# Two transformer blocks on one core: the order of the four products of a k-tile

## The chip, the cores and the metric

The kernel runs on one core of one Trainium2 chip. The metric is the device time of one execution in microseconds (us). TensorE (PE) does the matrix products, VectorE (DVE) and ScalarE (ACT) the elementwise work, and SyncE (SP) issues nearly all DMAs.

## The reference

Two transformer blocks follow each other on 256 tokens of width 2048, in float32. Nearly all the work is in products of the tokens with weight matrices:

```python
h = rmsnorm(x, norm_w[layer])
proj = h @ w_in[layer]
...
gm = jax.nn.sigmoid(h @ w_merge[layer] + b_merge[layer]).reshape(b, s, N_BRANCHES, D_MODEL)
merged = gm[:, :, 0] * y_a + gm[:, :, 1] * y_b
x = x + merged @ w_out[layer]
...
proj = xn @ w_in[l]
h = h + merged @ w_o[l]
hn = rmsnorm_2(h, ffn_norm_g[l])
up = causal_dwconv(hn @ w_up[l], ffn_conv_w[l], ffn_conv_b[l])
val, gt = jnp.split(up, 2, axis=-1)
h = h + (jax.nn.silu(gt) * val) @ w_down[l]
```

The first block has a pooling branch and a sparse attention, the second a convolution, a chunked attention and a memory attention, and a feed-forward part of width 5632. These parts are small beside the weight products.

## The kernel before

**Strips.** Each weight matrix is cut into strips of 256 output columns, and `stream` (L309) goes through all strips in one written-out list. A strip has one k-tile for each 128 rows of its matrix (16 for a matrix of 2048 rows; 2 to 24 occur). Weights arrive by DMA in granules of up to eight k-tiles (`raw` tiles). A step is up to four k-tiles of a granule: `split` (L349) has ACT round the raw weights to a `hi` tile (format fp32r, L168) and DVE compute `lo` = raw - hi (L172), two steps ahead of their use, into four `hi` and four `lo` buffers. The activations are split in the same way: a page `R` holds for a k-tile 256 columns of hi, one for each token, and behind them 256 columns of lo.

**The products.** In the mode "ws" (the weights stand in the array, the activations move through it) a k-tile has two halves `f` of 128 output columns each, with its own half `ps[:, f]` of the accumulator tile, 512 float32 columns. For each half there are two products, made by the helper `mm` (L204, so all of them are on L206): hi weights with all 512 columns of the page, and lo weights with its first 256. In this document "a hi" is the first of these, "a lo" the second. All k-tiles of a strip add into the same `ps`; `sum2` (L416) later adds the two column ranges of it. Two `ps` tiles take turns from strip to strip.

**The order.** The order on PE is the order in which the Python code calls `mm`; nothing reorders it (`manual_schedule`). `stream` issues a step's products, then calls `round` (L275), which lets the waiting epilogues and the attention jobs issue one piece each. In every k-tile but the last the order is hi, lo for half 0 and hi, lo for half 1. In a strip's last k-tile it is lo, hi, lo, hi, so that there two lo follow each other, and two hi follow each other where the next strip begins. The modes "as" (the activations stand, all products have 256 or 304 columns) and "cmp" are in the other branches of the same loop.

Of the kernel before, what the change touches and what calls it, by code (L numbers as in the profile page):

```python
# [72 lines left out]
class Builder:  # L73
# [235 lines left out]
    def stream(self, strips):  # L309
        steps, grans = [], []  # L310

        def granules(ss):
            for s in ss:
                kt = 0
                for ap, n in s.grans:
                    yield s, ap, n, kt
                    kt += n

        def order():
            for s in strips:  # L320
                if isinstance(s, Strip):
                    yield from granules([s])
                else:
                    runs = [granules(x) for x in s[:2]]
                    for i in s[2]:
                        yield next(runs[i])
        for s, ap, n, kt in order():
            for k0 in range(0, n, s.per):
                m = min(s.per, n - k0)
                steps.append((s, len(grans), k0, m, kt + k0, k0 + m >= n))  # L330
            grans.append((ap, n, s.width))
        raw, hl, loaded, done = {}, {}, 0, 0

        def cut(tile, n, w):
            return tile[:, 0:n * w].rearrange("p (k c) -> p k c", k=n)

        def load(most):
            nonlocal loaded
            while loaded < min(len(grans), most) and loaded - done < self.RAW:
                ap, n, w = grans[loaded]  # L340
                r = raw[loaded] = cut(self.t("raw", [128, 2048], self.RAW), n, w)
                if loaded:
                    self.dma(r[:, 0:n, :], ap)
                else:
                    self.dma(r[:, 0:4, :], ap[:, 0:4, :])
                    self.dma(r[:, 4:8, :], ap[:, 4:8, :])
                loaded += 1

        def split(j):  # L349
            nonlocal done  # L350
            s, g, k0, m, _, end = steps[j]
            h = cut(self.t("hi", [128, 1024], self.HL, F32R), m, s.width)
            l = cut(self.t("lo", [128, 1024], self.HL, F32R), m, s.width)
            self.split(h, l, raw[g][:, k0:k0 + m, :])
            hl[j] = h, l
            if end:
                del raw[g]
                done = g + 1

        for j in range(self.RAW):  # L360
            self.start_loads(j)
            load(j + 1)
        self.start_loads(self.RAW)
        for j in range(self.AHEAD):
            self.round()
            split(j)
        ended = None
        for j, (s, g, k0, m, kt, _) in enumerate(steps):
            if j + self.AHEAD < len(steps):
                split(j + self.AHEAD)  # L370
                load(len(grans))
            if kt == 0:
                self.drain(lambda: self.shared["ps"])
                s.ps = self.shared["ps"].popleft()
                if s.pre:
                    self.job(s.pre())
            self.drain(lambda: all(s.act(kt + q) is not None for q in range(m)))
            h, l = hl.pop(j)
            ps = s.ps
            for q in range(m):  # L380
                k = kt + q
                first, last = k == 0, k == s.nkt - 1
                x = s.act(k)
                if s.mode == "ws":
                    for f in range(2):
                        c = slice(f * 128, f * 128 + 128)
                        if last:
                            self.mm(ps[:, f, 0:256], l[:, q, c], x[:, 0:256], False, False)
                        self.mm(ps[:, f, :], h[:, q, c], x, first, last)
                        if not last:  # L390
                            self.mm(ps[:, f, 0:256], l[:, q, c], x[:, 0:256], False, False)
                elif s.mode == "as":
                    for f in range(2):
                        c, o = f * 128, ps[:, f, 0:s.width]
                        self.mm(o, x[:, c:c + 128], h[:, q, :], first, False)
                        self.mm(o, x[:, c:c + 128], l[:, q, :], False, False)
                        self.mm(o, x[:, 256 + c:384 + c], h[:, q, :], False, last)
                else:

                    if last:  # L400
                        self.mm(ps[0:60, 0, 0:256], x[:, 0:60], l[:, q, :], False, False)
                    self.mm(ps[0:120, 0, 0:256], x, h[:, q, :], first, last)
                    if not last:
                        self.mm(ps[0:60, 0, 0:256], x[:, 0:60], l[:, q, :], False, False)
            if ended is not None:
                self.job(ended)
                ended = None
            self.round()
            if kt + m == s.nkt:
                ended = s.epi(ps)  # L410
                if s.end:
                    s.end()
        self.job(ended)
        self.drain(lambda: not (self.epis or self.run or self.bg or self.fill))
# [1427 lines left out]
```

## Time and profile before

| | |
|---|---|
| median of 3 runs | 2566.55 us (2565.39 to 2566.99) |
| the profiled execution | 2566.05 us |
| its span, first to last instruction | 2564.3 us |
| PE busy | 2546.6 us, 99% |
| weight loads (PEld) busy | 2240.8 us, 87% |
| DVE busy | 1892.6 us, 74% |
| ACT busy | 1386.3 us, 54% |
| DMA | 481.24 MB, mean 188 GB/s |
| mean granted TensorE clock | 0.996 |

The span is the profiled execution's own; the 1.75 us between it and the execution's time lie around it. A busy share says how long an engine had at least one instruction in flight. PE's products overlap, and their ends are modelled, so what a product takes of PE's time is read from the starts.

### The profile page before, as it was taken

How to read it: one execution, taken by the hardware profiler on the slowest of the kernel's cores; microseconds unless marked ns; L12 is line 12 of the kernel's file. 1: busy time of each engine (PE TensorE's matmuls, PEld its weight loads, DVE VectorE, ACT ScalarE, POOL GpSimd, SP SyncE). 2: the span in 40 equal slices, each digit the busy share in tenths (PEclk: the TensorE clock that was granted, in tenths of full speed). 3: DMA queues.
4: the chain of work that ended last, by engine and by line, in shares of the span. 5: the costliest groups of instructions: out<-in, count | busy, mean ns of one | idle time of the engine just before them, and what ended most of it. 6: DMA issues, size and time to landing. Idle time of an engine off the chain costs nothing.

```text
span 2564.3 us, 37620 instructions
## 1 busy us (share of the span) xinstructions
PE 2546.6 (99%) x15126; PEld 2240.8 (87%) x15126; DVE 1892.6 (74%) x2990; ACT 1386.3 (54%) x2008; POOL 0.2 (0%) x4
## 2 busy tenths in 40 slices
PE   9999999999999999999999999999999999999997
PEld 7989888888888888888888888888888888888886
DVE  6687677777856667788888787677788764688764
ACT  6556555555554455555555445655555554455553
POOL 0000000000000000000000000000000000000000
PEclk9999999999999999999999999999999999999999
DMA  6757444444555566554555554555555555555553
GB/s 252 257 196 258 166 164 148 149 149 152 179 207 185 188 222 199 189 187 173 192 187 175 188 187 173 192 202 204 181 199 183 195 182 196 181 191 187 187 191 115
DMA packets 75632, 481.24 MB, mean 188 GB/s; under 512 B 8640, under 2 KB 8896, under 8 KB 20544
## 3 DMA queue, kind: packets, MB, share of 16 engines
q1 hardware_dynamic: 75024, 478.38, 52.9%
q8 instruction: 118, 1.93, 0.3%
q14 instruction: 58, 0.48, 0.1%
q10 hardware_dynamic: 432, 0.45, 0.1%
HBM read 472.50 MB, written 6.29 MB: 187 GB/s over the span
## 4 chain that ended last, share of the span: by engine, by line
PE 99%; DVE 1%; DMA 0%; ACT 0%; issue 0%; SPq 0%; DVEq 0%
PE ps L206 95%; PE A L206 2%; PE O L206 1%; PE A L216 1%; DMA raw<-in_w_mem 0%; DVE F L172 0%; DVE nq L172 0%; DVE lo L172 0%; ACT hi L168 0%; DVE F L187 0%; SPq L251 0%; DVE F L182 0%; DVE small L172 0%; ACT nq L168 0%; DVEq L1837 0%
## 5 line engine op out<-in xcount | busy, mean ns | idle before, releaser
L206 PE MATMUL ps<-R,hi 128*128 128x512 f32 x6480 | 2276.6, 396 | 2.2 <-ACT hi L168 2.2
L206 PE MATMUL ps<-R,lo 128*128 128x256 f32 x6480 | 1786.1, 281 | 0.5 <-DVE lo L172 0.5
L206 PEld LDWEIGHTS ps<-R,hi 128*128 128x128 f32 x6480 | 1208.7, 188 | 270.6 <-issue 3.2
L172 DVE TENSOR_TENSOR lo<-raw,hi 128x1024 fp32r<-128x1024 f32 (+1 forms) x878 | 1069.3, 1219 | 383.2 <-ACT hi L168 379.6
L206 PEld LDWEIGHTS ps<-R,lo 128*128 128x128 f32 x6480 | 1216.8, 188 | 18.8 <-DVE lo L172 1.0
L168 ACT ACTIVATE hi<-raw 128x1024 fp32r<-128x1024 f32 (+1 forms) x878 | 920.7, 1052 | 501.4 <-PE ps L206 386.5
L172 DVE TENSOR_TENSOR F<-ps,F 128x512 f32<-128x512 f32 (+1 forms) x226 | 155.0, 686 | 172.9 <-ACT F L168 158.6
L168 ACT ACTIVATE F<-ps 128x512 f32<-128x512 f32 (+1 forms) x210 | 124.8, 594 | 276.6 <-PE ps L206 276.4
L172 DVE TENSOR_TENSOR F<-F,F 128x512 f32<-128x512 f32 (+3 forms) x300 | 185.5, 620 | 8.7 <-ACT F L168 3.3
L182 DVE SCALAR_TENSOR_TENSOR F<-F,params,F 128x256 f32<-128x256 f32 (+2 forms) x424 | 188.4, 479 | 3.3
L206 PE MATMUL ps<-hi,R 128*128 128x256 f32 (+2 forms) x832 | 152.9, 281 | 0.1
L168 ACT ACTIVATE F<-F 128x256 f32<-128x256 f32 (+2 forms) x140 | 75.0, 535 | 117.2 <-DVE F L182 97.5
L206 PEld LDWEIGHTS ps<-hi,R 128*128 128x128 f32 (+1 forms) x832 | 129.7, 188 | 0.6 <-ACT hi L168 0.5
L168 ACT ACTIVATE F<-F,params 128x256 f32<-128x256 f32 x214 | 106.8, 545 | 31.8 <-DVE F L172 30.6
L206 PE MATMUL ps<-lo,R 128*128 128x256 f32 (+2 forms) x448 | 122.6, 280 | 0.0
L168 ACT ACTIVATE R<-F 128x256 fp32r<-128x256 f32 (+3 forms) x145 | 69.4, 490 | 54.8 <-DVE F L172 50.4
L206 PEld LDWEIGHTS ps<-lo,R 128*128 128x128 f32 (+1 forms) x448 | 80.6, 180 | 0.4
L172 DVE TENSOR_TENSOR R<-F,R 128x256 fp32r<-128x256 f32 (+3 forms) x129 | 62.1, 493 | 0.0
L182 DVE SCALAR_TENSOR_TENSOR F<-F,F 128x256 f32<-128x256 f32 (+1 forms) x112 | 60.7, 542 | 0.0
L168 ACT ACTIVATE R<-A 128x512 fp32r<-128x512 f32 (+2 forms) x56 | 29.8, 532 | 56.3 <-PE A L216 56.3
L172 DVE TENSOR_TENSOR R<-A,R 128x512 fp32r<-128x512 f32 (+2 forms) x56 | 34.0, 607 | 22.6 <-ACT R L168 22.6
L168 ACT ACTIVATE F<-F,mx 128x128 f32<-128x128 f32 (+1 forms) x96 | 42.7, 446 | 11.3 <-DVE mx L187 10.4
(101 smaller groups left out, 591.2 us busy)
## 6 DMA issues: line engine op xcount, KB each, us to landing
raw<-in_w_in SPq DMA_DIRECT2D x166, 1024.0 KB, 4.9
raw<-in_w_up SPq DMA_DIRECT2D x88, 1024.0 KB, 4.8
raw<-in_w_merge SPq DMA_DIRECT2D x32, 1024.0 KB, 4.8
raw<-in_w_down_a SPq DMA_DIRECT2D x24, 1024.0 KB, 4.8
raw<-in_w_nsa_out SPq DMA_DIRECT2D x16, 1024.0 KB, 4.9
raw<-in_w_out SPq DMA_DIRECT2D x16, 1024.0 KB, 5.3
raw<-in_w_o SPq DMA_DIRECT2D x16, 1024.0 KB, 4.8
raw<-in_w_down_b SPq DMA_DIRECT2D x16, 1024.0 KB, 4.8
```

The lines of the kernel that those rows point to most:

```text
L168: return self.nc.scalar.activation(out, in_, f, **k)
L172: return self.nc.vector.tensor_tensor(out, a, b, op=op)
L182: return self.nc.vector.scalar_tensor_tensor(out, a, s, b, op0=op0, op1=op1)
L206: return self.nc.tensor.matmul(out, l, r, start=start, stop=stop, skip_group_check=True)
L216: return self.nc.tensor.transpose(out, in_, self.ident[0:n, 0:n])
```

## The change

In the mode "ws" a k-tile's four products are now issued as hi for half 0, hi for half 1, lo for half 0, lo for half 1. This holds for the last k-tile of a strip as well, which had the lo ahead of the hi. The flag that opens an accumulation stays on the first k-tile's two hi, the one that closes it moves from the last k-tile's hi to its lo.

```diff
@@ -382,13 +382,11 @@
                 first, last = k == 0, k == s.nkt - 1
                 x = s.act(k)
                 if s.mode == "ws":
-                    for f in range(2):
-                        c = slice(f * 128, f * 128 + 128)
-                        if last:
-                            self.mm(ps[:, f, 0:256], l[:, q, c], x[:, 0:256], False, False)
-                        self.mm(ps[:, f, :], h[:, q, c], x, first, last)
-                        if not last:
-                            self.mm(ps[:, f, 0:256], l[:, q, c], x[:, 0:256], False, False)
+
+                    for w, n in ((h, 512), (l, 256)):
+                        for f in range(2):
+                            self.mm(ps[:, f, 0:n], w[:, q, f * 128:f * 128 + 128], x[:, 0:n],
+                                    first and n == 512, last and n == 256)
                 elif s.mode == "as":
```

The order of the instructions on PE, before, at the first products of the program (k-tile 0 of the first strip; `R_68` is the page of activations, and what a row waits for stands behind it):

```order
L206 MATMUL ps_120<-R_68,hi_175 128x512 [waits DVE_49,Activation_49]
L206 MATMUL ps_120<-R_68,lo_176 128x256 [waits DVE_49]
L206 MATMUL ps_120<-R_68,hi_175 128x512
L206 MATMUL ps_120<-R_68,lo_176 128x256
L206 MATMUL ps_120<-R_68,hi_175 128x512
```

And the same place on PE after the change:

```order
L206 MATMUL ps_120<-R_68,hi_175 128x512 [waits DVE_49,Activation_49]
L206 MATMUL ps_120<-R_68,hi_175 128x512
L206 MATMUL ps_120<-R_68,lo_176 128x256 [waits DVE_49]
L206 MATMUL ps_120<-R_68,lo_176 128x256
L206 MATMUL ps_120<-R_68,hi_175 128x512 x2
```

The wait for DVE, which makes the lo tile, moved from the second product to the third.

On PE before, where a strip ends (its last two k-tiles, page `R_75`) and the next one begins (page `R_68`, the other `ps` tile):

```order
L206 MATMUL ps_121<-R_75,hi_320 128x512
L206 MATMUL ps_121<-R_75,lo_321 128x256
L206 MATMUL ps_121<-R_75,hi_320 128x512
L206 MATMUL ps_121<-R_75,lo_321 128x256 x2
L206 MATMUL ps_121<-R_75,hi_320 128x512
L206 MATMUL ps_121<-R_75,lo_321 128x256
L206 MATMUL ps_121<-R_75,hi_320 128x512
L206 MATMUL ps_120<-R_68,hi_344 128x512 [waits Activation_49]
L206 MATMUL ps_120<-R_68,lo_345 128x256 [waits DVE_49]
```

The same place on PE after the change:

```order
L206 MATMUL ps_121<-R_75,hi_320 128x512 x2
L206 MATMUL ps_121<-R_75,lo_321 128x256 x2
L206 MATMUL ps_121<-R_75,hi_320 128x512 x2
L206 MATMUL ps_121<-R_75,lo_321 128x256 x2
L206 MATMUL ps_120<-R_68,hi_344 128x512 [waits Activation_49]
L206 MATMUL ps_120<-R_68,hi_344 128x512
L206 MATMUL ps_120<-R_68,lo_345 128x256 [waits DVE_49]
```

Products of one kind stand in pairs everywhere now, and a strip ends with two lo. On DVE, ACT and SP the instructions stand as before.

## Rows read from the trace of the kernel before

**Rows 1.** The page: span, TensorE's busy time, and the chain that ended last.

```profile
span 2564.3 us, 37620 instructions
...
PE 2546.6 (99%) x15126; PEld 2240.8 (87%) x15126; DVE 1892.6 (74%) x2990; ACT 1386.3 (54%) x2008; POOL 0.2 (0%) x4
...
PE 99%; DVE 1%; DMA 0%; ACT 0%; issue 0%; SPq 0%; DVEq 0%
PE ps L206 95%; PE A L206 2%; PE O L206 1%; PE A L216 1%; DMA raw<-in_w_mem 0%; DVE F L172 0%; DVE nq L172 0%; DVE lo L172 0%; ACT hi L168 0%; DVE F L187 0%; SPq L251 0%; DVE F L182 0%; DVE small L172 0%; ACT nq L168 0%; DVEq L1837 0%
```

**Rows 2.** Groups by line: count, busy us, mean ns, idle before, releaser.

```profile
L206 PE MATMUL ps<-R,hi 128*128 128x512 f32 x6480 | 2276.6, 396 | 2.2 <-ACT hi L168 2.2
L206 PE MATMUL ps<-R,lo 128*128 128x256 f32 x6480 | 1786.1, 281 | 0.5 <-DVE lo L172 0.5
L206 PEld LDWEIGHTS ps<-R,lo 128*128 128x128 f32 x6480 | 1216.8, 188 | 18.8 <-DVE lo L172 1.0
```

**Rows 3.** Timeline of TensorE, the first strip's end: start and duration in us.

```profile
23.42 0.39 PE L206 MATMUL ps<-R,hi 128*128 128x512 f32 x1
23.65 0.40 PE L206 MATMUL ps<-R,lo 128*128 128x256 f32 x2
23.89 0.39 PE L206 MATMUL ps<-R,hi 128*128 128x512 f32 x1
24.12 0.28 PE L206 MATMUL ps<-R,lo 128*128 128x256 f32 x1
24.24 0.62 PE L206 MATMUL ps<-R,hi 128*128 128x512 f32 x2
24.70 0.28 PE L206 MATMUL ps<-R,lo 128*128 128x256 f32 x1
```

**Rows 4.** Timeline of TensorE, the last place where one strip follows another.

```profile
2532.71 0.40 PE L206 MATMUL ps<-R,lo 128*128 128x256 f32 x2
2532.95 0.40 PE L206 MATMUL ps<-R,hi 128*128 128x512 f32 x1
2533.18 0.28 PE L206 MATMUL ps<-R,lo 128*128 128x256 f32 x1
2533.30 0.62 PE L206 MATMUL ps<-R,hi 128*128 128x512 f32 x2
2533.76 0.28 PE L206 MATMUL ps<-R,lo 128*128 128x256 f32 x1
```

**Rows 5.** Stretches: length, busy us (instructions) by engine, granted clock, DMA share, GB/s.

```profile
9.60:16.40 6.80, 6.28 (x18) 5.00 (x19) 5.74 (x9) 5.35 (x12) 0.00 (x0) 0.50 1.03 408
17.00:2552.00 2535.00, 2532.45 (x15096) 2232.44 (x15094) 1877.63 (x2960) 1375.94 (x1990) 0.00 (x0) 1.00 0.53 187
```

**Rows 6.** Timeline of the weight loads at the place of the fourth group.

```profile
2532.47 0.42 PEld L206 LDWEIGHTS ps<-R,lo 128*128 128x128 f32 x2
2532.83 0.19 PEld L206 LDWEIGHTS ps<-R,hi 128*128 128x128 f32 x1
...
2533.18 0.31 PEld L206 LDWEIGHTS ps<-R,hi 128*128 128x128 f32 x2
```

**Rows 7.** Timeline of TensorE, a chain of twelve 256-column products of an attention job.

```profile
1312.86 1.60 PE L206 MATMUL O<-R,R 128*128 128x256 f32 x12
```

**Rows 8.** Timeline of VectorE's first split and of TensorE at the program's start.

```profile
9.64 1.23 DVE L172 TENSOR_TENSOR lo<-raw,hi 128x1024 fp32r<-128x1024 f32 x1 [3.65 <-ACT hi L168]
...
9.66 0.80 PE L206 MATMUL ps<-R,hi 128*128 128x512 f32 x1 [2.16 <-ACT hi L168]
10.92 0.58 PE L206 MATMUL ps<-R,lo 128*128 128x256 f32 x1 [0.46 <-DVE lo L172]
11.30 0.63 PE L206 MATMUL ps<-R,hi 128*128 128x512 f32 x1
11.73 0.41 PE L206 MATMUL ps<-R,lo 128*128 128x256 f32 x1
```

**Rows 9.** Timeline of TensorE, the end of the last strip.

```profile
2547.63 0.40 PE L206 MATMUL ps<-R,lo 128*128 128x256 f32 x2
...
2548.22 0.40 PE L206 MATMUL ps<-R,hi 128*128 128x512 f32 x1
```

## The prediction

> **What bounds the kernel now.** I read the page first: the span is 2564.3 us, TensorE (PE) is busy in 99% of it, and the chain that ended last is 99% PE, 95% of it products into the `ps` tiles [rows 1]. So the time is the length of one queue of products. Next, the groups by line: 6480 products with a hi tile (512 columns) and 6480 with a lo tile (256 columns) are nearly all of that queue; they waited 2.2 us for ScalarE (ACT) and 0.5 us for VectorE (DVE) in the whole run [rows 2]. The change reorders exactly these 12960 products, four for each of 3240 k-tiles (6480 / 2). Their listed durations, 396 and 281 ns, can't be summed: they overlap. What a product takes of the queue is the space from its start to the next start, and that I read in the timeline: 0.23 us after a hi, 0.12 us after a lo [rows 3, 4]. The granted clock is full from 17 to 2552 us and half before it [rows 5].
>
> **The change, part by part.** Nothing is added or removed. Before, a k-tile is hi, lo (half 0), hi, lo (half 1); now it is hi, hi, lo, lo. The instructions of DVE, ACT and the DMA queue keep their order, and the load of each product's weights stays in front of it. So the question is whether the space after a product depends on its neighbour. The trace of before answers that, since all four kinds of neighbours stand in it: the last k-tile of a strip puts lo first, so at strip ends two lo follow each other, and then the strip's last hi is followed by the next strip's first hi. The first such place and the last where a strip follows another are in two groups of rows [rows 3, 4]. Between the first and last row shown there, with starts to the nanosecond and spaces over 300 ns left out, I averaged each kind:
>
> hi with a lo behind it: 231.3 ns (6123 places). hi with a hi behind it: 232.9 (166). lo with a hi behind it: 119.0 (6110). lo with a lo behind it: 118.6 (215). The medians are 231, 231, 119 and 118. [rows 3, 4]
>
> Before, a k-tile is 2 x 231.3 + 2 x 119.0 = 700.6 ns. By kinds alone, after is 232.9 + 231.3 + 118.6 + 119.0 = 701.8 ns. But the neighbour in front can be taken too. The second hi of a pair (hi in front, lo behind) was 230.5 ns (166 places), the second lo of a pair (lo in front, hi behind) 118.0 (215) [rows 3, 4]. So after is 232.9 + 230.5 + 118.6 + 118.0 = 700.0 ns: 0.6 ns less per k-tile, times 3240 = **-1.9 us**.
>
> Its bounds. Two of the four are uncertain. The 232.9 comes only from strip ends, where the second hi opens another strip; its median is the ordinary 231, so the real value may be 231.3. The last lo of a k-tile will now stand ahead of two hi's, which before only happens at a strip's last lo: 120.8 ns (166 places) [rows 3, 4]. Low end: 231.3 + 230.5 + 118.6 + 118.0 = 698.4, that is -2.2 x 3240 = -7.1 us. High end: 232.9 + 230.5 + 118.6 + 120.8 = 702.8, that is +2.2 x 3240 = +7.1 us. I take the value between them, because the 118.0 is a lo directly behind a lo, which is the larger part of the new situation, and because the 232.9 is at least measured on a pair.
>
> **Weight loads.** A load row lasts 188 ns [rows 2], and a load begins with the product ahead of its own, so the load under a lo has only 119 ns until its product starts. In the new order two such short covers stand in a row where now they alternate with long ones. If a load had to wait for the end of the one before, the second lo would run out of cover: two loads need 376 ns, two lo's give 238, and 138 ns x 3240 would be 447 us. The rows exclude it: at a strip's end the loads of two hi's together take 0.31 us, so the second begins 0.31 - 0.19 = 0.12 us after the first, and the load of the hi at 2532.83 begins before the lo's ahead of it end at 2532.47 + 0.42 = 2532.89 [rows 6]; and twelve 256-column products in one chain took 1.60 us, or (1.60 - 0.28) / 11 = 0.12 us from start to start, with a load for each [rows 7]. So loads overlap each other, and order costs nothing there. The Trainium skill, page "TensorE: Matmul & The Clock Gate", section "LDWEIGHTS (loading the stationary operand)", gives a load as its columns divided by 1.2 GHz; as an estimate that is 107 ns for 128 columns, not 188, which would fit under any 119 ns lo and leave the sum as it is; the 0.12 us spacing agrees with that and not with the listed 188.
>
> **Waits.** Each step's first lo is needed one hi later than now (0.23 us), and its hi tiles are read for the last time one lo earlier (0.12 us). Both go toward more slack. It is worth something at one place, the first product of the program: there hi starts at 9.66, and the lo that follows waits for DVE's split, which ends at 9.64 + 1.23 = 10.87, until 10.92. Now the second hi goes into that hole. At the half clock granted there a hi takes 11.73 - 11.30 = 0.43 us [rows 5, 8], so **-0.4 us**, with 0 as the other bound if the next steps' splits are then late. At the end, the last k-tile's four products take the same total and its last product is 256 columns with 0.28 us listed instead of 512 with 0.40: starting at 2547.75 (the second of the two lo's at 2547.63), hi, hi, lo, lo puts the last start at 2547.75 + 2 x 0.23 + 0.12 = 2548.33 and its end at 2548.61, now 2548.22 + 0.40 = 2548.62 [rows 9]: nothing. The tail behind it, all of it in sequence on DVE, is untouched.
>
> **Sum.** -1.9 - 0.4 = -2.3 us on the profiled execution's 2566.05 us, whose span of 2564.3 leaves 1.75 around it. The median of the runs is 2566.55, 0.5 above it; the forecast for the median is 2566.55 - 2.3 = **2564.3 us**, 0.09% less. A measurement of this kernel can tell about 0.2%, 5.1 us, from no change, so this is "no change".
>
> **Rivals.**
> *Faster: the order has a real gain.* If the hi ahead of a hi is the ordinary 231.3 and the other three keep their pair values, each k-tile loses 2.2 ns: 2566.55 - 7.1 - 0.4 = 2559.0 us. For it: the medians, and that strip ends carry other things than order. Against it: the gain is put together from differences of 0.8, 0.4 and 1.0 ns, each measured at strip ends alone. It decides from 1.5 ns per k-tile on, (5.1 - 0.4) / 3240.
> *Slower: hi behind hi costs at both of its ends.* A lo ahead of two hi's was 1.8 ns longer than an ordinary one, and a hi ahead of a hi 1.6 ns longer. If that comes from two 512-column products in a row and not from the strip's end, it is paid at every k-tile: +2.2 ns each, 2566.55 + 7.1 - 0.4 = 2573.3 us. For it: both differences show in 166 places. Against: a lo cannot well be held up by the product after the next, the hi spaces at strip ends have the ordinary median, and a strip's end is where the other `ps` tile is taken. The point from which it decides: 1.7 ns per k-tile, (5.1 + 0.4) / 3240.
> *The order is not what counts at all*, and PE's spaces stay at 700.6 ns: 2566.1 us with the start's 0.4. That is the same outcome as mine.
>
> **How the numbers follow.** My forecast together with the third case has 0.75, the faster rival 0.13, the slower one 0.12. The two rivals' times, 2559.0 and 2573.3, are also the ends that the unknown costs give; the runs themselves spread by 1.6 us, so the range is 2558.0 to 2574.0. For the likeliest case alone it is 2561.5 to 2569. Faster by over 0.2% (below 2561.4): the faster rival and little else, 0.14. Slower by over 0.2% (above 2571.7): 0.11. Within: 0.75.
>
> **What would show it.** In the profile after, the groups have the same counts (6480 and 6480) and no new wait. The timeline shows hi x2 and lo x2, 0.46 us between the start of a hi pair and its lo pair, 0.24 us from there to the next hi pair. The first lo starts at 10.92 as now, with a second hi in front of it. A k-tile of 698.4 ns would speak for the faster rival, one of 702.8 for the slower one, and the space after the first hi (231.3 or 232.9) and after the last lo (118.0 or 120.8) would say which of the two bounds holds. The prediction is wrong if the spaces after a hi or a lo differ from all those of the strip ends, say because long runs of pairs do something that a single pair did not, or if PE shows idle time in front of the first hi or the first lo of a step.

## The result and the profile after

The changed kernel took 2533.14 us (median of 4 runs, 2532.08 to 2534.39), beside 2565.97 us for the kernel before (4 runs, 2564.81 to 2566.99): ratio 0.9872, 95% interval 0.9855 to 0.9889. It is faster by 33 us, outside the forecast's range.

The page of the kernel after, and its groups by line (columns as in [rows 2]); they answer to [rows 1, 2]:

```profile
span 2530.4 us, 37620 instructions
...
PE 2513.9 (99%) x15126; PEld 2226.9 (88%) x15126; DVE 1890.3 (75%) x2990; ACT 1385.4 (55%) x2008; POOL 0.2 (0%) x4
```

```profile
L206 PE MATMUL ps<-R,hi 128*128 128x512 f32 x6480 | 2019.6, 393 | 0.6 <-ACT hi L168 0.6
L206 PE MATMUL ps<-R,lo 128*128 128x256 f32 x6480 | 1279.8, 279 | 0.8 <-DVE lo L172 0.8
```

TensorE is still the bound, with the same 12960 products; their waits are 0.6 us for ACT and 0.8 us for DVE, no more in sum than before. The groups' busy times fell by hundreds of us, but that is only that products of one kind now overlap each other; the gain is in the starts. The timeline of TensorE after, in the middle of a late strip (start, duration):

```profile
2200.46 0.62 PE L206 MATMUL ps<-R,hi 128*128 128x512 f32 x2
2200.92 0.40 PE L206 MATMUL ps<-R,lo 128*128 128x256 f32 x2
2201.15 0.62 PE L206 MATMUL ps<-R,hi 128*128 128x512 f32 x2
2201.61 0.39 PE L206 MATMUL ps<-R,lo 128*128 128x256 f32 x2
...
2202.53 0.62 PE L206 MATMUL ps<-R,hi 128*128 128x512 f32 x2
```

Three k-tiles from 2200.46 to 2202.53, 0.690 us each. The same moment of the kernel before, the first hi of each k-tile, in a stretch that is slower than its average:

```profile
2199.79 0.39 PE L206 MATMUL ps<-R,hi 128*128 128x512 f32 x1
...
2200.49 0.40 PE L206 MATMUL ps<-R,hi 128*128 128x512 f32 x1
...
2201.20 0.40 PE L206 MATMUL ps<-R,hi 128*128 128x512 f32 x1
...
2201.91 0.39 PE L206 MATMUL ps<-R,hi 128*128 128x512 f32 x1
...
2202.61 0.40 PE L206 MATMUL ps<-R,hi 128*128 128x512 f32 x1
```

2202.61 - 2199.79 = 2.82 us for four, 0.705 us each; the average before was 0.7006. To the nanosecond, from the starts and averaged over the run, the four spaces of the order after are 227.8 (hi ahead of hi; 3136 places), 230.5 (hi ahead of lo; 3211), 116.7 (lo ahead of lo; 3212) and 115.5 ns (lo ahead of hi; 3074): 690.5 ns per k-tile, not the forecast 700.0. Three of the four are shorter than they were at the strip ends; the hi ahead of a lo is the same. 700.6 - 690.5 = 10.1 ns x 3240 = 33 us: these spaces hold the whole gain. A little was lost elsewhere: the products with standing activations, which nobody touched, took 1.4 us more (152.5 us after, 151.1 before).

The spaces are not scattered; they repeat. Before, a stretch of k-tiles repeats 231, 117, 234, 123, 237, 118 ns, or 232, 119, 229, 120, 229, 118. After, it repeats 231, 114, 113, 226, 229, 120, 117, 230, from the second hi of a k-tile on. So a step (four k-tiles) takes one of a few values. Of some 670 steps that no other product interrupts, 359 took 697 or 698 ns per k-tile before, 116 took 700 or 701, 112 took 705 or 706, 25 took 708; after, 620 of 670 took 690. I call such a repeating pattern a lock.

The start, which answers to [rows 8]:

```profile
7.75 0.94 PE L206 MATMUL ps<-R,hi 128*128 128x512 f32 x2
9.01 0.51 PE L206 MATMUL ps<-R,lo 128*128 128x256 f32 x2 [0.32 <-DVE lo L172]
...
12.17 0.73 PE L206 MATMUL ps<-R,hi 128*128 128x512 f32 x2 [0.59 <-ACT hi L168]
```

In this execution the first weights came 1.9 us earlier than in that of [rows 8], and the granted clock was full here; the second strip began 3.1 us earlier. From there to the last hi or lo it is 2523.8 us before and 2493.1 after, 30.6 less. Repeated, the order after began at 10.08, again with the full clock, and took 2534.15 us, so the start is worth no more than a microsecond or two of the 33.

### The profile page after: what moved, and what is told of

Read it like the earlier page. It is cut to its first block, busy times and chain, and to the rows that moved or that the text cites. A ratio compares the mean times of both kernels' runs of the same rounds, so it can differ in the third digit from the quotient of the medians.

```text
span 2530.4 us, 37620 instructions
## 1 busy us (share of the span) xinstructions
PE 2513.9 (99%) x15126; PEld 2226.9 (88%) x15126; DVE 1890.3 (75%) x2990; ACT 1385.4 (55%) x2008; POOL 0.2 (0%) x4
## 4 chain that ended last, share of the span: by engine, by line
PE 99%; DVE 1%; DMA 0%; ACT 0%; SPq 0%; issue 0%; DVEq 0%
PE ps L206 94%; PE A L206 2%; PE O L206 2%; PE A L216 1%; DMA F<-in_memT 0%; DVE F L172 0%; ACT R L168 0%; SPq L251 0%; DVE nq L172 0%; DVE lo L172 0%; DVE F L187 0%; ACT hi L168 0%; DVE F L182 0%; DVE small L172 0%; ACT nq L168 0%
## 5 line engine op out<-in xcount | busy, mean ns | idle before, releaser
L206 PE MATMUL ps<-R,hi 128*128 128x512 f32 x6480 | 2019.6, 393 | 0.6 <-ACT hi L168 0.6
L206 PE MATMUL ps<-R,lo 128*128 128x256 f32 x6480 | 1279.8, 279 | 0.8 <-DVE lo L172 0.8
L206 PEld LDWEIGHTS ps<-R,hi 128*128 128x128 f32 x6480 | 983.5, 188 | 7.6 <-issue 3.2
```

Of the source, the lines that this page charges most:

```text
L206: return self.nc.tensor.matmul(out, l, r, start=start, stop=stop, skip_group_check=True)
```

## The experiments

Each average below is 2 x the mean space after a hi + 2 x that after a lo, from 30 us on, spaces over 300 ns left out; "k-tile" is this sum. It is 700.8 ns before and 690.6 after. The first six edits replace the loop over a step's products by a list of (k-tile, half, hi or lo). The listings show only the lines that matter; PAIRS stands for a list written out in the kernel.

**Which property of the order counts?** The order after once more; the halves in another sequence; long and short alternating again with other halves; pairs that do not stream the same page.

```diff
 # a_repeat
+todo = [(q, f, hi) for q in range(m) for f, hi in ((0, 1), (1, 1), (0, 0), (1, 0))]
 # b_banks
+todo = [(q, f, hi) for q in range(m) for f, hi in ((0, 1), (1, 1), (1, 0), (0, 0))]
 # c_lengths, d_moving: if kt, in place of the list of a_repeat
+todo = [(p + q, f, hi) for p in range(0, m, 2) for q, f, hi in PAIRS]
+c_lengths: PAIRS = 0 0 hi, 0 1 lo, 1 0 hi, 1 1 lo, 0 1 hi, 0 0 lo, 1 1 hi, 1 0 lo
+d_moving:  PAIRS = 0 0 hi, 1 1 hi, 0 0 lo, 1 1 lo, 1 0 hi, 0 1 hi, 1 0 lo, 0 1 lo
```

> The changed order once more (hi 0, hi 1, lo 0, lo 1; the same instructions in the same order as the changed kernel), as the yardstick for the runs beside it. Every theory: about 2533 us, 690 ns per k-tile. The theory of a locked phase says more: in the strips whose activations stand, where no instruction was changed, the space between starts was 113.3 ns in some strips and 117.8 ns in others, not the same ones before and after; if that is set by where a strip happens to start and not by its code, this run may show another mix of the two, with the same instructions.

> The order hi 0, hi 1, lo 1, lo 0 in every k-tile: long and short products stand in the same places as in the changed kernel and every pair reads the same activations, but the third product adds into the half that the second has just written, and the next k-tile's first into the half of this one's last. Theory A (a product behind one into the same accumulator half costs some 5 ns; before there were two such in a k-tile, after none): two again, so the gain is gone, about 2566 us. Theory B (two products of one length in a row are cheaper) and theory C (two products in a row that stream the same columns are cheaper): 2533 us as the changed kernel. Theory D (no price for a pair; the spaces depend on the phase that the whole repeated order locks into): a value of its own, anywhere between 2520 and 2570.

> Over two k-tiles q and q+1: hi 0 of q, lo 1 of q, hi 0 of q+1, lo 1 of q+1, then hi 1 of q, lo 0 of q, hi 1 of q+1, lo 0 of q+1; a strip's first step (four k-tiles) keeps the changed order. Long and short alternate as before the change, but only two of eight products follow one into the same accumulator half (before: four of eight). Theory A: half to all of the gain stays in the altered k-tiles, about 2540 to 2545 us. Theory B: the alternation is what costs, so only the first steps keep the gain, about 2558 us (2533 + 3/4 of 33). Theory C: every second product still streams the first columns of the page just read, as before, 2558 us. Theory D: a value of its own.

> Over two k-tiles q and q+1: hi 0 of q, hi 1 of q+1, lo 0 of q, lo 1 of q+1, hi 0 of q+1, hi 1 of q, lo 0 of q+1, lo 1 of q; a strip's first step keeps the changed order. Lengths and accumulator halves stand as in the changed kernel, but no product streams the columns that the one ahead of it has streamed. Theory A and theory B: 2533 us. Theory C (the gain is that a pair streams the same columns): the altered three quarters lose it, about 2558 us. Theory D: a value of its own.

Measured: 2534.15 us (ratio to before 0.9877, interval 0.9861 to 0.9894), 2534.46 (0.9878, 0.9863 to 0.9893), 2567.97 (1.0009, 0.9999 to 1.0018), 2534.17 (0.9877, 0.9862 to 0.9892). Theories A (the accumulator half) and C (the same streamed columns) fall: b_banks and d_moving keep all of the gain. What counts is how long and short products alternate. But a fixed price of alternating, theory B, does not give c_lengths: the first steps of its strips, which kept the changed order, kept most of the gain (151 of 187 took 690 to 694 ns per k-tile), and the altered steps were slower than the kernel before with its 700.6 (398 of 483 took 705 to 708), though long and short alternate in both. And the strips with standing activations, whose instructions nobody touched: the first 240 of their products stood 113.3 ns apart in the kernel before, 113.4 in c_lengths, and 117.8 in the four kernels with pairs; a later group of 96 stood 117.8 apart in the kernel before and in those four, and 113.3 in c_lengths. The same code has two values, and only what ran ahead of it differs.

**Longer runs, and products alone.**

```diff
 # e_runs4
+todo = [(p + q, f, hi) for p in range(0, m, 2) for hi in (1, 0) for q in range(2) for f in range(2)]
 # f_runs8
+todo = [(q, f, hi) for hi in (1, 0) for q in range(m) for f in range(2)]
 # m_bench: no kernel, one tile of activations and one of weights
+for n in seq("hl", 240): mm(*ops(n))       # and hhll, hhhlll, ..., h, l
+for n in [128] * 1: mm(*ops(n))            # shifts the start
+for n in seq("hl", 240): mm(*ops(n))       # and hhll, l
```

> Runs of four: over two k-tiles the four hi, then the four lo (halves 0 and 1 in turn). The change of length from one product to the next now comes half as often as in the changed kernel, a quarter as often as before. Theory B1 (each change between a long and a short product costs; four per k-tile before, two after, 10.1 ns apart, so 5 ns each): one per k-tile, 5 ns less again, 2533 - 16 = 2517 us. Theory B2 (it is enough that a product has a neighbour of its own length, so all of the gain is there with pairs): 2533 us. Theory D (the phase that the order locks into): a value of its own; the spaces will repeat in a pattern of their own, and no sum of prices gives it.

> Runs of eight: all hi of a step (four k-tiles), then all its lo. One change of length for two k-tiles. Theory B1: 7.5 ns per k-tile less than the changed kernel, 2533 - 24 = 2509 us. Theory B2: 2533 us. Theory D: a value of its own, not on a line with the runs of one, two and four.

> Products alone: one tile of activations, one of weights, no other engine at work, nothing of the two blocks is computed. Sequences of 240 products of 512 columns (h) and 240 of 256 (l), each on a line of its own: h l alternating, in pairs, in threes, fours and eights, 480 h alone, 480 l alone; then h l, h h l l and l alone again behind one or three products of 128 columns that shift the start; then both orders with weights of 64 columns, and both in bf16. Theory B1 and B2 (a price in the array or the weight loads): the real kernel's difference is here too, alternating about 175 ns per product (350 per pair of h and l), in pairs 172.5; B1: falling further with the length of the runs, B2: not. If the other engines' traffic makes the difference, both orders are equal here. Theory D: the same order takes another time behind a shifted start, l alone above all (113 or 118 ns per product, as the strips with standing activations showed). If the weight load takes part, the 64-column weights, whose load is shorter, shrink the difference.

Measured: e_runs4 2537.25 us (0.9892, 0.9877 to 0.9907; k-tile 691.9), f_runs8 2531.19 us (0.9868, 0.9852 to 0.9885; k-tile 690.2, its steps at 685 or 693). f_runs8 is the fastest version run, by 2 us under the changed kernel; their intervals overlap. Theory B1, a price per change of length, falls: it wanted 2517 and 2509. B2 fits these two within 4 us. It falls in m_bench: there, from start to start, h and l alternating took 346.7 ns per pair of products from 23.88 us on, and the same sequence took 353.3 further on, behind one product of 128 columns and again behind three more, against 348.3 in pairs. (Behind the first one the halves are exchanged; behind all four they are not.) The same instructions have two speeds, one on either side of the paired order. Runs of three, four and eight took 350.0, 350.8 and 349.2. Theory D had expected two speeds of l alone above all: it took 120.0 ns per product behind every start. With weights of 64 columns alternating took 340.0 and pairs 350: the width of the weights takes part. Whether it acts through their load or through the 64 output rows, these rows do not separate. In bf16 both orders took 325.0 to 325.4. The Trainium skill, page "TensorE: Matmul & The Clock Gate", section "Back-to-back issue gap", gives N / 2.4 + 2.5 ns from start to start for N columns at the full clock, as the gap of matmuls without their weight loads; for 512 and 256 columns that is an estimate of 325.0 ns per pair, which these bf16 rows meet, with loads, and no fp32r stretch does.

**Is it the start?** Both orders in turn behind 0 to 7 products of 128 columns, in the form of the strips; and one such product at the head of each strip of the real kernel.

```diff
 # n_bench
+for o, w, a, s in ktiles("before", 40): mm(o, w, a, start=s, stop=True)
+for o, w, a, s in shift(n): mm(...)        # n = 0 to 7, between the stretches
 # g_shift_after, h_shift_before; i_uniform_before is the latter without these lines
+if kt == 0:
+    self.mm(ps[:, 0, 0:128], h[:, 0, 0:128], s.act(0)[:, 0:128], True, True)
```

> Products alone in the form of the real strips (a hi and a lo tile of weights, a page of activations, two accumulator halves that are added into), nothing of the two blocks is computed: stretches of 40 k-tiles in the order of before and of after in turn, each behind 0 to 7 products of 128 columns that shift where it starts; then hi alone, lo alone, and both orders with weights of 64 columns. Theory D (an order locks into a phase, which it has several of): the order of before takes different times in its stretches, among 693, 698, 701 and 707 ns per k-tile, and keeps one time for long parts of a stretch; the order of after takes fewer values, 690 above all. A rival, E: the real kernel's several values come from the other engines' and the DMAs' traffic; then each order has one value here, whatever the shift. With 64-column weights the loads are shorter: if they take part, the values change.

> The order of before (hi 0, lo 0, hi 1, lo 1, in the last k-tile too) with one product more at the head of every strip: 128 columns into the accumulator, which the next product overwrites. About 165 products more of 60 to 110 ns, 10 to 18 us if nothing else moves. Theory D: the strips start elsewhere, so the share of the steps at 698, 701, 706 and 708 ns per k-tile changes against the run without that product; the time moves by more or less than the 10 to 18 us. Theory E, or a fixed price per pair: the shares stay, and the time is that of the run without it plus 10 to 18 us.

> The order of before in every k-tile, the last one of a strip included (before the change that one had lo ahead of hi). The control for the run with one product more per strip, and the change's other part alone: the last k-tile's order. A fixed price per pair: 2566 us within 1. Theory D: near 2566, with another mix of 698, 701, 706 and 708 ns among the steps.

> The order of after with the same one product more at the head of every strip. Theory D with one strong lock: the steps stay at 690 ns per k-tile, and the time is 2533 us plus 10 to 18 us, some 2543 to 2551 us. If the 690 ns were an accident of where the strips start, many steps would leave it, and the time would go towards 2566 us and over.

In n_bench the order of before took 693.3 ns per k-tile behind 0, 3 and 7 products and 706.7 behind 1, 2, 4, 5 and 6, from some k-tiles after the head on; the order of after 696.7 behind all eight. No other engine worked, so theory E (traffic) falls. The 690 that theory D had expected of the order of after did not come. The timeline of n_bench at the heads and ends of two stretches of 40 k-tiles in the order of before (L62, L70):

```profile
126.86 0.45 PE L62 MATMUL ps<-page,hi 128*128 128x512 f32 x1
...
155.16 0.34 PE L64 MATMUL ps<-page,hi 128*128 128x128 f32 x2
...
183.54 0.44 PE L70 MATMUL ps<-page,hi 128*128 128x512 f32 x1
...
211.33 0.45 PE L72 MATMUL ps<-page,hi 128*128 128x128 f32 x3
```

28.30 us for the first, 27.79 for the second, of the same instructions; two products and three stood ahead.

In the real kernel: i_uniform_before 2572.44 us (1.0027, 1.0015 to 1.0038). It alters nothing but the last k-tile of a strip, and loses 6.5 us, and its steps lock elsewhere: 705 to 708 in 342 of 670 steps instead of 137. h_shift_before 2599.16 us (1.0128, 1.0098 to 1.0157), g_shift_after 2563.89 us (0.9990, 0.9979 to 1.0001). The 10 to 18 us for the added products were too low; there are 216 of them, not 165. In g_shift_after, groups and timeline:

```profile
L206 PE MATMUL ps<-R,hi 128*128 128x128 f32 x216 | 50.2, 232 | 3.8 <-ACT hi L168 3.8
```

```profile
1295.69 0.74 PE L206 MATMUL ps<-R,hi 128*128 128x128 f32 x3
1296.27 0.40 PE L206 MATMUL ps<-R,lo 128*128 128x256 f32 x2
```

The added product and the two hi behind it take 0.58 us to the first lo, where two hi take 0.46. In starts it is 58 ns at most heads, and then 286 instead of 230 for the first hi: the load of that hi's weights had only 58 ns of cover. In n_bench products of 128 columns, each with its load, stood 109 to 115 ns apart behind one another, so the load, not the columns, seems to set the space. 114 ns x 216 = 25 us. What is left over is 26.7 - 25 = 2 us against i_uniform_before and 30 - 25 = 5 us against a_repeat. In g_shift_after it is at the head too: the way from a strip's last product to the first hi of the next became 72 ns longer on average, not 58, and a strip's second k-tile took 703.4 ns instead of 689.5. From the third k-tile on the strips ran as in a_repeat, 688 and 692 ns in turn, 690 on average. So the time went to 2564 us, as the expectation had it for an accident of the start, but the steps did not leave the 690: the order after finds back to this lock within two k-tiles.

**Why 690 here and 697 alone?** First with other engines at work and with eight pages and four weight buffers in turn, then with the operands at ten placements in memory.

```diff
 # p_bench: 20 each beside a stretch; pages[k // 2 % 8], his[k // 4 % 4]
+nc.vector.tensor_tensor(big[:, 2, :], big[:, 0, :], big[:, 1, :], op=mybir.AluOpType.subtract)
+nc.scalar.activation(big2[:, 2, :], big2[:, 0, :], AF.Copy)
 # q_bench, r_bench: weights and page begin wat and pat elements further on
+m, c, p = (512 if h else 256), wat + k % 4 * 256 + f * 128, pat + k % 2 * 512
```

> Products alone once more, 48 k-tiles a stretch, both orders in turn behind 0 to 3 products of 128 columns; nothing of the two blocks is computed. First with one page and one pair of weight buffers, then with VectorE and ScalarE running full-width copies and subtractions beside it for some 24 us of each stretch, then with eight pages and four weight buffers in turn as in the real kernel, then with both. It asks why the real kernel's values (690 ns for the order of after; 698, 701, 706, 708 for that of before) are others than those of the products alone (697; 693 and 707). If the addresses set them: the third part shows 690 and 698. If the other engines' traffic does: the second part, while it runs. If neither: all four parts show 697, and 693 or 707, and what else differs in the real kernel (the DMAs' writes, the semaphores at each step, the jobs between the steps) stays open.

> Products alone, 32 k-tiles a stretch, both orders in turn behind 0, 1 and 3 products of 128 columns, and all that for ten placements in memory: weights and page both at a multiple of 128 bytes, then the weights 16, 32, 64, 128, 960 and 192 bytes further on, the page 64 or 32 bytes further on, and both 64. In the real kernel the pages begin at a multiple of 128 bytes and the hi and lo buffers 64 bytes past one; in the earlier runs of products alone both began at a multiple. Theory F (where the weights lie sets which phases an order can lock into): with the weights 64 bytes on, the order of before shows the real kernel's 698, 701, 706 or 708 ns per k-tile and the order of after its 690; with 0 or 128 it shows 693, 707 and 697. If all ten placements show 693, 707 and 697, addresses have no part in it.

p_bench: in every stretch the order of before locks at 693.3 or 706.7 and that of after at 696.7, with the engines at work or not, with one buffer or many. q_bench shows what does it. The first product of neighbouring stretches of 32 k-tiles without a shift, weights 0 (L48, L50), 16 (L68, L70) and 960 bytes on (L148, L150); in each pair the order of before comes first:

```profile
30.22 0.40 PE L48 MATMUL ps<-page,hi 128*128 128x512 f32 x1
...
52.83 0.40 PE L50 MATMUL ps<-page,hi 128*128 128x512 f32 x1
...
75.14 0.22 PE L52 MATMUL ps<-page,hi 128*128 128x128 f32 x1
...
165.44 0.39 PE L68 MATMUL ps<-page,hi 128*128 128x512 f32 x1
...
187.63 0.39 PE L70 MATMUL ps<-page,hi 128*128 128x512 f32 x1
...
210.23 0.22 PE L72 MATMUL ps<-page,hi 128*128 128x128 f32 x1
...
707.44 0.40 PE L148 MATMUL ps<-page,hi 128*128 128x512 f32 x1
...
730.06 0.40 PE L150 MATMUL ps<-page,hi 128*128 128x512 f32 x1
...
752.15 0.22 PE L152 MATMUL ps<-page,hi 128*128 128x128 f32 x1
```

Before and after: 22.61 and 22.31 us; 22.19 and 22.60; 22.62 and 22.09. The built program places the real kernel's hi buffers 960 bytes past a page's place modulo 4096 (64 past a multiple of 128). At that placement, and equally at 192 bytes or with the page 64 further on, products alone show the real kernel's values: 690.0 for the order of after, 706.7 or 697.8 for that of before. At 16 bytes the order of before is the faster one, 693.3 against 706.7, from all three starts. With weights and page both 64 bytes further on, the values of 0 come back (696.7; 693.3 or 706.7, behind other starts), so, as far as this one pair shows, the distance between the two counts and not the place of each. Nor is 128 the period: at 64 bytes the order of after took 693.3, not 690.0, and at 128 that of before took 702.2, while 192 and 960, which are equal modulo 256, agree. So in the real kernel:

```diff
 # j_pad_after, k_pad_before: raw, hi and lo move by 64 bytes, to a multiple of 128
-        self.small = self.one.tile([128, 124], F32, name="small")
+        self.small = self.one.tile([128, 140], F32, name="small")
 # l_16_before, l_16_after: hi and lo 16 bytes past a multiple of 128 (for lo alike)
-            h = cut(self.t("hi", [128, 1024], self.HL, F32R), m, s.width)
+            h = cut(self.t("hi", [128, 1056], self.HL, F32R)[:, 20:1044], m, s.width)
```

> The changed kernel with one small tile made 64 bytes longer, so that the raw, hi and lo buffers behind it begin at a multiple of 128 bytes and the pages stay; no instruction is added or moved. Theory F: the steps lock at the 697 ns of the products alone instead of 690, 6.7 ns x 3240 = +22 us, about 2555 us, and most of the gain is gone. If addresses have no part: 2533 us.

> The kernel before the change with the same 64 bytes. Theory F: the steps lock at 693 or 707 ns instead of 698, 701, 706 and 708; half and half would be 700 ns and about the 2566 us of now, all at 693 about 2545 us, all at 707 about 2590 us, and by the theory the order of before may beat the order of after here. If addresses have no part: 2566 us and the old mix.

> Products alone, 32 k-tiles a stretch, the orders of before, of after and in runs of eight, each with the weights 0, 8, 16 and so on to 120 bytes past a multiple of 128 and once 4 bytes past it, the page at a multiple. Theory F: each order has a value or two for each placement, 690 to 707 ns per k-tile, and which order is the better one changes with the placement; at 64 bytes after is 690 to 693 and runs of eight 685 to 693, at 0 after is 697. If a placement gives the order of after or the runs of eight less than 685 ns, it is the one to run in the real kernel; if none does, the real kernel's 64 bytes are about as good as a placement gets.

> The kernel before the change with the hi and lo weights moved to 16 bytes past a multiple of 128 (they were 64 bytes past one), by longer buffers of which a part is used; no instruction is added or moved. Products alone at 16 bytes took 693.3 ns per k-tile in the order of before, from every start. Theory F: 700.6 - 693.3 = 7.3 ns x 3240 = 24 us less than 2566, about 2542 us. If the placement had no part in the real kernel: 2566 us.

> The changed kernel with the weights 16 bytes past a multiple of 128. Products alone at 16 bytes took 706.7 ns per k-tile in the order of after. Theory F: 706.7 - 690.5 = 16.2 ns x 3240 = 52 us more than 2533, about 2585 us, and the change of order would have made this kernel slower, by 43 us. If the sign of the gain belongs to the order and not to the placement, it stays below the other run, near 2533 us.

Measured: j_pad_after 2557.72 us (0.9969, 0.9956 to 0.9981; k-tile 696.8, 619 of 670 steps at 696 or 697). 64 bytes cost the changed kernel 24 us. k_pad_before 2578.60 us (1.0051, 1.0036 to 1.0066; k-tile 702.9): they cost the kernel before 13 us, so at this placement the change of order is worth 21 us and not 33. r_bench, one start for each of 17 placements and three orders: 693 to 707 ns; the order of after is the faster in 8 placements, that of before in 6, and in 3 they are within 1 ns of each other. These counts are of one start: at 32 bytes the order of before took 693.3 here, and 706.7 from all three starts of q_bench. l_16_before 2557.53 us (0.9966, 0.9953 to 0.9979; k-tile 697.5) and l_16_after 2576.56 us (1.0041, 1.0026 to 1.0055; k-tile 703.6): **with the weights 16 bytes past a multiple of 128 the same change makes the kernel 19 us slower.** The times were 16 us above and 8 us below the forecasts, 2542 and 2585. One reason may be the edit: a buffer of 1056 elements is 128 bytes longer, so every second hi and lo buffer lies 16 + 128 = 144 bytes past the page modulo 256, a placement that no run of products alone had. That this explains the rest is not shown. l_16_after, then l_16_before, on TensorE in a late strip:

```profile
2200.35 0.64 PE L206 MATMUL ps<-R,hi 128*128 128x512 f32 x2
2200.82 0.40 PE L206 MATMUL ps<-R,lo 128*128 128x256 f32 x2
2201.06 0.63 PE L206 MATMUL ps<-R,hi 128*128 128x512 f32 x2
```

```profile
2199.89 0.39 PE L206 MATMUL ps<-R,hi 128*128 128x512 f32 x1
2200.12 0.28 PE L206 MATMUL ps<-R,lo 128*128 128x256 f32 x1
...
2200.58 0.39 PE L206 MATMUL ps<-R,hi 128*128 128x512 f32 x1
```

0.71 us for a k-tile in pairs, 0.69 alternating: the picture of the kernels before and after with the roles exchanged.

## Why the prediction was wrong

- **The bound** was right: one queue of products on TensorE, before and after, and starts, not durations, are what to sum.
- **The step that failed** is the one that took a product's space from its neighbours: "So after is 232.9 + 230.5 + 118.6 + 118.0 = 700.0 ns". The four numbers are right for strip ends, but a strip's end is one irregular place in a repeating pattern and shows that pattern's disturbance. The 166 places of the 232.9 were not even alike: 78 took 236 or 237 ns and 75 took 229 to 231, so the mean stood between two groups, and the median of 231 hid them. In the run of pairs the four are 227.8, 230.5, 116.7 and 115.5, together 9.5 ns less than forecast, 31 us. The prediction's last sentence names this case, that long runs of pairs do something that a single pair did not, but gave it no price and no chance.
- **The bounds**, -7.1 and +7.1 us, were made of the same numbers, so they could not hold it. An honest bound was in the trace of before: its own steps took 697 to 708 ns per k-tile in the same code, 11 ns x 3240 = 36 us from end to end. Its strips with standing activations had runs of 256-column products 113.3 ns apart and others 117.8 apart, and its chains in the attention jobs 120 [rows 7].
- **The faster rival** had the right sign and named the right doubt, that strip ends carry other things than order, but with -7.1 us a fifth of the size. The slower rival's mechanism, hi ahead of hi, was not there: that space became shorter.
- **Weight loads**: that a load needs little more than 100 ns of cover held (286 - 230 = 56 ns too late under a product of 58). "Order costs nothing there" is open: with 64-column weights the values of both orders changed, so the loads may take part in the lock.
- **Waits and the start** were right in kind: the second hi runs while the first lo is split, and the one wait behind it, 0.59 us for the next step's hi, was named as a possibility. The -0.4 us can't be told from the profiles, whose clocks differ at the start.

That the sequence of long and short lengths, the start and the placement together set the time is shown by runs. By what path the placement and the start act is not: no trace shows it, and it stays open.

## What to carry to other kernels

Where fp32r products bind and the starts repeat in a pattern, a price measured at the pattern's breaks can't be carried into its middle; look for the same instructions at two speeds in the trace, and take the spread as the bound. Judge an order of products at several placements of its operands, by moving a buffer by 16 to 64 bytes, before the gain is put down to the order: here the same edit gave -33 us, -21 or +19. A gain of this kind is to be measured again after each change of the memory layout.

## What the runs showed of the hardware

- The same sequence of fp32r products has more than one steady speed; which one it takes depends on what ran ahead of it (693.3 or 706.7 ns per k-tile, 2%), and it then keeps it for the whole stretch.
- 64 bytes of placement are worth 24 us of 2533 in a kernel whose memory traffic is otherwise the same. In products alone the distance from weights to page counts: with both moved by 64 bytes the values were those of 0 again.
- The steady patterns listed here are each a whole number of 6.67 ns (16 cycles of 2.4 GHz) long: 690.0 x 2 = 207 of them, 693.3 = 104, 696.7 x 2 = 209, 706.7 = 106, 680.0 (two pairs of 340.0 with 64-column weights) = 102. In bf16, 325.0 ns, it is not.
- VectorE and ScalarE at full width beside the products changed no space by as much as 0.1 ns on average.
